# Decoder trunk on one core: x laid out by features, key/query before gates, unit matrix moved by 96 bytes

## The chip, the cores and the metric

The kernel runs on one core of one Trainium2 chip. The time is device microseconds of one execution, the median of three runs. A separate execution was profiled; it has its own time and a span, which is the part between the first and the last instruction that the profiler recorded. Engines are called TensorE (PE, with PEld for its weight loads), VectorE (DVE), ScalarE (ACT), GpSimd (POOL) and SyncE (SP, which here only starts transfers).

## The reference, cut to what matters

Two decoder layers on 256 tokens of 2048 features, all in float32: a gated DeltaNet mixer, a SwiGLU network, an HGRN2 mixer, a SwiGLU network, and a last norm. The change touches how the first mixer begins:

```python
h = x
h = h + gdn_mixer(rmsnorm(h, gdn_norm[j]), gdn_w_in[j], ...)

def gdn_mixer(h, w_in, conv_w, a_log, dt_bias, head_norm, w_out):
    proj = h @ w_in                       # q, k, v | z | b, a
    qkv = silu(causal_depthwise_conv(proj[..., :GDN_CONV_DIM], conv_w))
    ...
    beta = sigmoid(b)
    g = -exp(a_log) * softplus(a + dt_bias)
    o = gated_delta_rule_chunked(q, k, v, beta, g)
    o = rmsnorm(o, head_norm) * silu(z)
    return o @ w_out
```

The norm's weights are folded into x in front of the products (`split_scaled`), and the norm's scale of each token (rstd, one over the root of the mean square) is applied behind them.

## The kernel before, in words

**Products in three parts.** A float32 product is made of three faster ones. Each operand is split into a high part, in a shorter format, and the low rest: x into `xt_h` and `xt_l`, weights into `wh` and `wl`. TensorE then sums wh·xh, wh·xl and wl·xh. The high part is written by ScalarE (`activation` with Copy), the low part by VectorE (raw minus high).

**The stream.** All weights pass once through `stream`, in halves of 128 x 1024 numbers (512 KB): SP loads `raw` (four buffers), ScalarE writes `wh`, VectorE writes `wl` (four buffers each), TensorE multiplies. Halves are laid out in groups; a group is one set of output columns with an accumulator `main` (two of them, used in turn), and its `end` function takes the result out. A high or low part can be written only once TensorE has finished with the half four places earlier, and a group can start only once the accumulator of two groups earlier has been emptied. The order of the groups of the DeltaNet stage is the string `GDN_ORDER`: k0 is the key/query group of heads 0, then k1 and so on, v the values, z the output gate, o the output projection. In front of k0 stands the group `ba`, one half with the 64 columns of the gates b and a. A key/query half is 24 matmuls with 256 columns of x moving (`mm_cols`), a half of v, z or o is 12 matmuls with 512 columns of weights moving (`mm_rows`), and the gates' half is 48 matmuls of 256 columns (`mm_gates`).

**How x comes in.** `start` loads x in four pieces of 512 columns, tokens on partitions. TensorE transposes each piece (`make_xt`, eight transposes of 128 x 128 with the unit matrix `head` moving), ScalarE and VectorE split what comes out, scaled by the norm's weights. ScalarE sums the squares of the same pieces (`sumsq`, output in `junk`), and `make_rstd` makes the scales: a short chain over VectorE, GpSimd (power -0.5), VectorE (the scale times the unit matrix, in `vjunk`) and TensorE (`ones` times that), so that `rstd_row` holds the scales of all tokens on every partition. Ten matmuls of `ones` come first, to keep TensorE busy until x is there.

**What the groups' ends do.** `gates_end` makes decay and beta from the gates' group, a chain over VectorE, ScalarE and DRAM (`g_rows`, `g_tots`, read back on all partitions). `kq_end` empties the accumulator into `pre` times `rstd_row` (`conv_evac`), runs the convolution and its SiLU (`gdn_qk`), makes `dec`, the decay between tokens, on ScalarE in 24 pieces of 128 x 64 and one exponential over all of them, and starts the triangular inverse (`gdn_inverse`), a long chain of small VectorE steps on `u`. `z_end` calls `gdn_o`, whose matmuls are the small products `aux<-r,u`, `aux<-w,nmat` and `aux<-w,dec`; square sums of their result follow on ScalarE (`junk<-aux`), then the transposes `aux<-head,zs`.

**What sets the order.** Nothing is issued as it is written. Every operation is recorded with its inputs, outputs and an estimated cost, and `plan` lays out one order for each engine from these costs and from how late an operation may come; main matmuls keep the order of the stream, all other work is put between. `lag` is the estimated time to landing of a transfer, `edge` forces one operation behind another. All instructions are issued from one line (490), so the profile's groups are told apart by the names of their tiles.

**Where constants lie.** `setup` lays out the constants one behind the other in the order of the calls. `head`, which holds the unit matrix and the norms' weights, lies at byte 128 modulo 512 of each partition; `wh` in row groups and most work tiles lie at 32.

Of the kernel before, what the change touches and what calls it, by code (L numbers as in the profile page):

```python
# [17 lines left out]
P = 128  # L18
T = 256
# [487 lines left out]
class Trunk:  # L507
# [27 lines left out]
    def setup(self):  # L535
        nc, c = self.nc, self.const
        t = lambda shape, tag, dt=F32: self.tile(c, shape, tag, dt)
        self.x_home = self.tile(self.dram, [T, D], "x_home", bufs=1)
        self.x_at, self.x = self.a["x"], {}
        head = t([P, P + 64], "head")  # L540
        nc.sync.dma_start(head, self.a["head"])
        nc.ops[-1].lag = 2.4
        self.queue = [nc.ops[-1]]
        self.ident = head[:, 0:P]
        self.norms = head[:, P : P + 64].rearrange("p (n c) -> p n c", n=4)
        self.ones = t([P, P], "ones")
        nc.gpsimd.memset(self.ones, 1.0)
        self.neghalf = t([P, 8], "neghalf")
        nc.gpsimd.memset(self.neghalf, -0.5)
        self.rstd = t([P, 2], "rstd")  # L550
        self.rstdh = t([P, 2], "rstdh")
        self.rstd_row = t([P, T], "rstd_row")
        self.ssp = t([P, 2, 4], "ssp")
        self.ss = t([P, 2], "ss")
        self.junk = t([P, 512], "junk")
        self.vjunk = t([P, 256], "vjunk")
        self.xt_h = [t([P, 4, T], f"xt_h{i}", F32R) for i in range(4)]
        self.xt_l = [t([P, 4, T], f"xt_l{i}", F32R) for i in range(4)]

    def start(self, norm, row):  # L560

        pool = self.nc.pool("first", 1, phase=True)
        for cg in range(4):
            if cg < 2:
                self.x[cg] = self.tile(pool, [P, 2, 512], f"first{cg}")
            else:
                self.x[cg] = self.tile(self.xpool, [P, 2, 512], "x", ordered=True)
            self.nc.sync.dma_start(self.x[cg], self.x_cols(self.x_at, cg))
            self.nc.ops[-1].lag = (2.5, 2.2, 3.0, 3.0)[cg]
            self.nc.edge(self.queue[-1], self.nc.ops[-1])  # L570
            self.queue.append(self.nc.ops[-1])
        warm = self.aux()
        for i in range(10):
            self.nc.tensor.matmul(
                warm[:, (i % 4) * P : (i % 4 + 1) * P], self.ones, self.ones, start=True, stop=True
            )
        for cg in range(4):
            self.make_xt(cg, norm)
        for cg in range(4):
            self.nc.after(self.xt_h[cg])  # L580
            self.sumsq(cg)
        self.nc.close(pool)
        self.make_rstd(row)


# [1 line left out]
    def stream(self, groups):  # L587
        nc = self.nc
        flat = [(g, i) for g in groups for i in range(len(g.halves))]
        ready = {}  # L590

        def place(tag, g):
            w = self.tile(self.wsplit, [P, 1024], tag, F32R, ordered=True)
            v = nc.virtual(w)
            v.pad, v.cols = PAD, g.cols
            return w

        def load(n):
            g, i = flat[n]
            raw = self.tile(self.wraw, [P, 1024], "raw", ordered=True)  # L600
            nc.sync.dma_start(raw, g.halves[i])
            if n == 0:
                nc.ops[-1].lag = 4.2
                nc.edge(self.queue[1], nc.ops[-1])
            h = place("wh", g)
            nc.scalar.activation(h, raw, AF.Copy)
            low = place("wl", g)
            nc.vector.tensor_tensor(out=low, in0=raw, in1=h.bitcast(F32), op=ALU.subtract)
            ready[n] = (h, low)

        loaded = 0
        for n, (g, i) in enumerate(flat):
            while loaded < min(n + AHEAD, len(flat)):
                load(loaded)
                loaded += 1
            if i == 0:
# [34 lines left out]

    def mm_cols(self, ps, i, wh, wl, n_k, n_f, n_chunks):

        for k in range(n_k):
            kt = i * n_k + k
            xh, xl = self.operand(kt)
            for f in range(n_f):
                at = (k * n_f + f) * P
                for m, (w, s) in enumerate(((wh, xh), (wh, xl), (wl, xh))):
                    self.nc.tensor.matmul(  # L660
                        ps[:, f // 2, (f % 2) * T : (f % 2 + 1) * T], w[:, at : at + P], s,
                        start=(kt == 0 and m == 0 and f % 2 == 0),
                        stop=(i == 2 * n_chunks - 1 and k == n_k - 1 and m == 2),
                        skip_group_check=True,
                    )

    def mm_gates(self, ps, i, wh, wl):
        for kt in range(16):
# [573 lines left out]
    def gdn_o(self, hg, st):  # L1242
# [39 lines left out]
    def gdn(self, after):  # L1282
        a = self.a
        states = [{} for _ in range(N_HG)]
        groups = []

        def gates_end(ps):
            self.gdn_gates(ps)

        ba = Group([a["gdn_ba"]], self.mm_gates, gates_end)  # L1290
        cols = lambda chunks, end: Group(
            chunks, lambda ps, i, h, l: self.mm_cols(ps, i, h, l, 2, 4, 4), end, cols=True
        )

        def part(hg):
            st = states[hg]

            def kq_end(ps):
                self.gdn_qk(hg, self.conv_evac(ps), st)
                self.gdn_inverse(hg, st)  # L1300

            def v_end(ps):
                self.gdn_v(hg, ps, st)

            def z_end(ps):
                st["zs"] = zs = self.tile(self.pool, [P, 2, 512], "zs", bufs=2)
                for tt in range(2):
                    self.nc.scalar.activation(
                        zs[:, tt, :], ps[:, tt, :], AF.Silu, scale=self.rstd[:, tt : tt + 1]
                    )  # L1310
                self.gdn_o(hg, st)
# [12 lines left out]
        groups.insert(0, ba)  # L1324
        groups[0].begin = self.gdn_setup
        return groups

# [332 lines left out]

    def run(self):
        self.setup()
        self.start(0, True)
        groups = self.gdn(self.next_input(1, False))
        groups += self.ffn(0, self.next_input(2, True))
        groups += self.hgrn(self.next_input(3, False))
        groups += self.ffn(1, self.finish)
        self.stream(groups)
        self.leave()
# [12 lines left out]
def layout(inputs):  # L1682
    f = lambda n: np.ascontiguousarray(inputs[n])
    out = {}
    x = f("x").reshape(T, D)
    out["x"] = np.ascontiguousarray(x.reshape(2, P, 4, 512).transpose(2, 1, 0, 3))
    cols = lambda v: v.reshape(16, P).T
    ffn_norm = f("ffn_norm")
    norms = [cols(v) for v in (f("gdn_norm")[0], ffn_norm[0], f("hgrn_norm")[0], ffn_norm[1])]
# [18 lines left out]
    w = f("gdn_w_in")[0]  # L1708
# [4 lines left out]
    ba = w[:, 6 * D :].reshape(16, P, 64)  # L1713
# [47 lines left out]
```

## Time and profile before

| | us |
|---|---|
| median of three runs | 2769.14 (2768.69 to 2769.49) |
| profiled execution | 2768.12 |
| its span | 2766.0 |
| TensorE matmuls, busy | 2749.6 |
| TensorE weight loads, busy | 2333.5 |
| VectorE busy | 1899.9 |
| ScalarE busy | 1428.6 |
| GpSimd busy | 251.6 |

The granted TensorE clock of the profiled execution is 0.999 of full speed. In the rows, `out<-in` names the tiles, `x8` the number of instructions merged, and a note in brackets the idle time in front of them with what ended it. Rows of the transfers end with the median time from issue to landing. A matmul is recorded longer than the distance to the next one, since they are pipelined; the distance is what counts. Rows of a chain of waits are start, length, engine and tile. Rows of stretches give, for each engine in the order PE, PEld, DVE, ACT, POOL, its busy time, then the granted clock, the transfer engines' busy share and GB/s.

### The profile page before, as it was taken

How to read it: one execution, taken by the hardware profiler on the slowest of the kernel's cores; microseconds unless marked ns; L12 is line 12 of the kernel's file. 1: busy time of each engine (PE TensorE's matmuls, PEld its weight loads, DVE VectorE, ACT ScalarE, POOL GpSimd, SP SyncE). 2: the span in 40 equal slices, each digit the busy share in tenths (PEclk: the TensorE clock that was granted, in tenths of full speed). 3: DMA queues.
4: the chain of work that ended last, by engine and by line, in shares of the span. 5: the costliest groups of instructions: out<-in, count | busy, mean ns of one | idle time of the engine just before them, and what ended most of it. 6: DMA issues, size and time to landing. Idle time of an engine off the chain costs nothing.

```text
span 2766.0 us, 41091 instructions
## 1 busy us (share of the span) xinstructions
PE 2749.6 (99%) x15662; PEld 2333.5 (84%) x15662; DVE 1899.9 (69%) x2857; ACT 1428.6 (52%) x2010; POOL 251.6 (9%) x370
## 2 busy tenths in 40 slices
PE   9999999999999999999999999999999999999998
PEld 9888888888888888888888989988888888888887
DVE  7787888877766667446675688778657675456764
ACT  6646666565554444344444556556454444344443
POOL 1213222232110000000000100000100000000000
PEclk9999999999999999999999999999999999999999
DMA  7686668687776666676667655555776666766664
GB/s 262 201 282 222 189 213 286 205 276 218 229 254 202 193 194 194 224 223 195 192 191 224 219 163 175 168 166 176 231 258 195 193 193 209 224 208 194 195 200 160
DMA packets 162677, 580.52 MB, mean 210 GB/s; under 512 B 20138, under 2 KB 21306, under 8 KB 162352
## 3 DMA queue, kind: packets, MB, share of 16 engines
q1 hardware_dynamic: 138912, 503.15, 57.0%
q0 software_dynamic: 23280, 73.91, 8.5%
q8 instruction: 122, 2.00, 0.3%
q10 hardware_dynamic: 288, 0.85, 0.1%
q14 instruction: 75, 0.61, 0.1%
HBM read 550.52 MB, written 27.31 MB: 209 GB/s over the span
## 4 chain that ended last, share of the span: by engine, by line
PE 99%; ACT 0%; DVE 0%; issue 0%; DMA 0%; SPq 0%; POOLq 0%; POOL 0%; ACTq 0%
PE main L490 92%; PE aux L490 6%; ACT dec L490 0%; DMA first<-in_x 0%; DVE wl L490 0%; ACT wh L490 0%; DVE utmp L490 0%; SPq L490 0%; DVE pre L490 0%; ACT xt_h L490 0%; DVE u L490 0%; ACT y L490 0%; POOLq L1757 0%; ACT junk L490 0%; DVE xl L490 0%
## 5 line engine op out<-in xcount | busy, mean ns | idle before, releaser
L490 DVE TENSOR_TENSOR wl<-raw,wh 128x1024 fp32r<-128x1024 f32 x945 | 1160.7, 1229 | 755.6 <-ACT wh L490 742.2
L490 ACT ACTIVATE wh<-raw 128x1024 fp32r<-128x1024 f32 x945 | 1000.8, 1060 | 1226.9 <-PE main L490 1126.3
L490 PE MATMUL main<-wh,xt_h 128*128 128x512 f32 x2176 | 849.3, 390 | 0.8 <-ACT wh L490 0.8
L490 PE MATMUL main<-wl,xt_h 128*128 128x512 f32 x2176 | 848.4, 390 | 1.3 <-DVE wl L490 1.3
L490 PE MATMUL main<-wh,xt_l 128*128 128x512 f32 x2176 | 849.5, 390 | 0.0
L490 PEld LDWEIGHTS main<-wl,xt_h 128*128 128x128 f32 x2176 | 408.5, 188 | 85.7 <-DVE wl L490 1.6
L490 PEld LDWEIGHTS main<-wh,xt_h 128*128 128x128 f32 x2176 | 408.5, 188 | 85.0 <-ACT wh L490 1.2
L490 PEld LDWEIGHTS main<-wh,xt_l 128*128 128x128 f32 x2176 | 408.6, 188 | 84.4
L490 PE MATMUL main<-xt_h,wh 128*128 128x256 f32 (+1 forms) x1040 | 290.5, 279 | 0.7 <-ACT wh L490 0.7
L490 PE MATMUL main<-xt_h,wl 128*128 128x256 f32 (+1 forms) x1040 | 290.1, 279 | 1.0 <-DVE wl L490 0.9
L490 PE MATMUL main<-xt_l,wh 128*128 128x256 f32 (+1 forms) x1040 | 290.0, 279 | 0.3 <-DVE xt_l L490 0.3
L490 PE MATMUL main<-wh,htl 128*128 128x512 f32 x664 | 258.6, 389 | 0.0
L490 PE MATMUL main<-wl,hth 128*128 128x512 f32 x664 | 258.3, 389 | 0.0
L490 PE MATMUL main<-wh,hth 128*128 128x512 f32 x664 | 258.3, 389 | 0.0
L490 PEld LDWEIGHTS main<-xt_h,wl 128*128 128x128 f32 (+1 forms) x1040 | 194.5, 187 | 1.5 <-DVE wl L490 1.4
L490 PEld LDWEIGHTS main<-xt_h,wh 128*128 128x128 f32 (+1 forms) x1040 | 194.5, 187 | 1.3 <-ACT wh L490 0.9
L490 PEld LDWEIGHTS main<-xt_l,wh 128*128 128x128 f32 (+1 forms) x1040 | 194.5, 187 | 1.0 <-DVE xt_l L490 0.5
L490 DVE STREAM_TRANSPOSE turned<-h 32x256 f32<-32x256 f32 x352 | 153.5, 436 | 7.2
L490 PE MATMUL main<-wh,ot_l 128*128 128x512 f32 x384 | 151.2, 394 | 0.0
L490 PE MATMUL main<-wh,ot_h 128*128 128x512 f32 x384 | 150.6, 392 | 0.0
L490 PE MATMUL main<-wl,ot_h 128*128 128x512 f32 x384 | 150.5, 392 | 0.0
L490 PEld LDWEIGHTS main<-wh,hth 128*128 128x128 f32 x664 | 124.7, 188 | 25.9
(206 smaller groups left out, 2249.0 us busy)
## 6 DMA issues: line engine op xcount, KB each, us to landing
raw<-in_ffn_gu SPq DMA_DIRECT2D x352, 512.0 KB, 4.7
raw<-in_ffn_d SPq DMA_DIRECT2D x176, 512.0 KB, 4.7
raw<-in_hgrn_in SPq DMA_DIRECT2D x128, 512.0 KB, 4.1
raw<-in_gdn_kq SPq DMA_DIRECT2D x64, 512.0 KB, 5.4
raw<-in_gdn_v SPq DMA_DIRECT2D x64, 512.0 KB, 4.7
raw<-in_gdn_z SPq DMA_DIRECT2D x64, 512.0 KB, 4.9
raw<-in_gdn_out SPq DMA_DIRECT2D x64, 512.0 KB, 5.0
x_home<-x POOLq DMA_DIRECT2D x36, 512.0 KB, 6.7
```

What stands on the lines that cost most here:

```text
L490: getattr(getattr(tc.nc, op.eng), op.method)(*args, **kw)
```

## The change

It has four parts.

1. A second copy of x, laid out by features (`x_turned`), comes as an input. `start` loads it in four pieces and splits it straight away; the 32 opening transposes go, and ten warm-up matmuls become nine. The pieces of x with tokens on partitions are still loaded, for the square sums and the residual, behind the turned ones.
2. The first four halves of the stream are issued by `start`, each in front of a piece of turned x, in one forced order on SP.
3. k0 comes first in the stream and the gates' group second; of k0's end, only the emptying of the accumulator stays there, and the rest (`gdn_qk`, `gdn_inverse`) is held back until the gates' end has been recorded. In the very first half, the matmuls are sorted: all wh·xh, then all wl·xh, then all wh·xl.
4. The constants are laid out in another order, with two of them widened (`neghalf` to 72 columns, `vjunk` to 320), so that `head` lies at byte 32 modulo 512. `ones`, `junk`, `vjunk` and `rstd_row` come to lie at 288; all tiles behind the constants keep their place modulo 512.

```diff
@@ setup
+        neghalf = t([P, 72], "neghalf")
+        self.neghalf = neghalf[:, 0:8]
...
         head = t([P, P + 64], "head")
-        nc.sync.dma_start(head, self.a["head"])
-        nc.ops[-1].lag = 2.4
-        self.queue = [nc.ops[-1]]
...
+        self.vjunk = t([P, 320], "vjunk")[:, 0:256]
+        self.queue = []
+        self.in_turn(head, self.a["head"], 2.4)
...
+    opening = True
+
+    def in_turn(self, out, in_, lag):
+        self.nc.sync.dma_start(out, in_)
+        op = self.nc.ops[-1]
+        op.lag = lag
+        if self.queue:
+            self.nc.edge(self.queue[-1], op)
+        self.queue.append(op)
+
-    def start(self, norm, row):
+    def start(self, norm, row, first):
...
         for cg in range(4):
-            if cg < 2:
-                self.x[cg] = self.tile(pool, [P, 2, 512], f"first{cg}")
-            else:
-                self.x[cg] = self.tile(self.xpool, [P, 2, 512], "x", ordered=True)
-            self.nc.sync.dma_start(self.x[cg], self.x_cols(self.x_at, cg))
...
+            raw = self.tile(self.wraw, [P, 1024], "raw", ordered=True)
+            self.in_turn(raw, first[cg], 3.0)
+            self.early.append(raw)
+            turned.append(self.tile(pool, [P, 4, T], f"first{cg}"))
+            self.in_turn(turned[cg], self.a["x_turned"][cg], 3.0)
         warm = self.aux()
-        for i in range(10):
+        for i in range(9):
...
         for cg in range(4):
-            self.make_xt(cg, norm)
+            for k in range(4):
+                self.split_scaled(
+                    self.xt_h[cg][:, k, :], self.xt_l[cg][:, k, :], turned[cg][:, k, :],
+                    self.norms[:, norm, 4 * cg + k : 4 * cg + k + 1],
+                )
+        nc.close(pool)
         for cg in range(4):
-            self.nc.after(self.xt_h[cg])
+            self.x[cg] = self.tile(self.xpool, [P, 2, 512], "x", ordered=True)
+            self.in_turn(self.x[cg], self.x_cols(self.x_at, cg), 4.0)
             self.sumsq(cg)
-        self.nc.close(pool)
         self.make_rstd(row)
@@ mm_cols
+        steps = [(k, f, m) for k in range(n_k) for f in range(n_f) for m in range(3)]
+        if self.opening:
+            steps.sort(key=lambda s: -s[2] % 3)
+            self.opening = False
...
@@ gdn
         def gates_end(ps):
             self.gdn_gates(ps)
+            held.pop()()
...
             def kq_end(ps):
-                self.gdn_qk(hg, self.conv_evac(ps), st)
-                self.gdn_inverse(hg, st)
+                pre = self.conv_evac(ps)
+
+                def rest():
+                    self.gdn_qk(hg, pre, st)
+                    self.gdn_inverse(hg, st)
+
+                if hg:
+                    rest()
+                else:
+                    held.append(rest)
...
-        groups.insert(0, ba)
+        groups.insert(1, ba)
@@ run
-        self.start(0, True)
         groups = self.gdn(self.next_input(1, False))
+        self.start(0, True, groups[0].halves)
@@ layout
+    out["x_turned"] = np.ascontiguousarray(x.T.reshape(4, 4, P, T).transpose(0, 2, 1, 3))
```

More of the change, by code (lines that the diff above doesn't have):

```diff
@@ L539, in setup @@
         self.x_at, self.x = self.a["x"], {}
+        neghalf = t([P, 72], "neghalf")
+        self.neghalf = neghalf[:, 0:8]
+        self.rstd = t([P, 2], "rstd")
+        self.rstdh = t([P, 2], "rstdh")
+        self.ssp = t([P, 2, 4], "ssp")
+        self.ss = t([P, 2], "ss")
         head = t([P, P + 64], "head")
-        nc.sync.dma_start(head, self.a["head"])
-        nc.ops[-1].lag = 2.4
-        self.queue = [nc.ops[-1]]
         self.ident = head[:, 0:P]
@@ L546, in setup @@
         self.ones = t([P, P], "ones")
-        nc.gpsimd.memset(self.ones, 1.0)
[L548 to L556, printed above, removed]
+        self.rstd_row = t([P, T], "rstd_row")
@@ L557, in setup @@
+        self.junk = t([P, 512], "junk")
+        self.vjunk = t([P, 320], "vjunk")[:, 0:256]
+        self.queue = []
+        self.in_turn(head, self.a["head"], 2.4)
+        nc.gpsimd.memset(self.ones, 1.0)
+        nc.gpsimd.memset(neghalf, -0.5)
         self.xt_h = [t([P, 4, T], f"xt_h{i}", F32R) for i in range(4)]
         self.xt_l = [t([P, 4, T], f"xt_l{i}", F32R) for i in range(4)]
-    def start(self, norm, row):
-        pool = self.nc.pool("first", 1, phase=True)
-        for cg in range(4):
-            if cg < 2:
-                self.x[cg] = self.tile(pool, [P, 2, 512], f"first{cg}")
-            else:
-                self.x[cg] = self.tile(self.xpool, [P, 2, 512], "x", ordered=True)
-            self.nc.sync.dma_start(self.x[cg], self.x_cols(self.x_at, cg))
-            self.nc.ops[-1].lag = (2.5, 2.2, 3.0, 3.0)[cg]
-            self.nc.edge(self.queue[-1], self.nc.ops[-1])
-            self.queue.append(self.nc.ops[-1])
+    opening = True
@@ new lines, in in_turn @@
+    def in_turn(self, out, in_, lag):
[6 more added lines that the diff above has]
+    def start(self, norm, row, first):
+        nc = self.nc
+        pool = nc.pool("first", 1, phase=True)
+        self.early = []
+        turned = []
+        for cg in range(4):
+            raw = self.tile(self.wraw, [P, 1024], "raw", ordered=True)
[3 more added lines that the diff above has]
+            self.in_turn(turned[cg], self.a["x_turned"][cg], 3.0)
@@ L572, in start @@
         warm = self.aux()
-        for i in range(10):
-            self.nc.tensor.matmul(
+        for i in range(9):
+            nc.tensor.matmul(
                 warm[:, (i % 4) * P : (i % 4 + 1) * P], self.ones, self.ones, start=True, stop=True
@@ L599, in load @@
             g, i = flat[n]
[L600 to L604, printed above, removed]
+            if n < len(self.early):
+                raw = self.early[n]
+            else:
+                raw = self.tile(self.wraw, [P, 1024], "raw", ordered=True)
+                nc.sync.dma_start(raw, g.halves[i])
             h = place("wh", g)
@@ L652, in mm_cols @@
     def mm_cols(self, ps, i, wh, wl, n_k, n_f, n_chunks):
-        for k in range(n_k):
+        steps = [(k, f, m) for k in range(n_k) for f in range(n_f) for m in range(3)]
+        if self.opening:
+            steps.sort(key=lambda s: -s[2] % 3)
+            self.opening = False
+        for k, f, m in steps:
             kt = i * n_k + k
             xh, xl = self.operand(kt)
[L657 to L665, printed above, removed]
+            w, s = ((wh, xh), (wh, xl), (wl, xh))[m]
+            at = (k * n_f + f) * P
+            self.nc.tensor.matmul(
+                ps[:, f // 2, (f % 2) * T : (f % 2 + 1) * T], w[:, at : at + P], s,
+                start=(kt == 0 and m == 0 and f % 2 == 0),
+                stop=(i == 2 * n_chunks - 1 and k == n_k - 1 and m == 2),
+                skip_group_check=True,
+            )
     def mm_gates(self, ps, i, wh, wl):
@@ L1285, in gdn @@
         groups = []
+        held = []
         def gates_end(ps):
             self.gdn_gates(ps)
+            held.pop()()
         ba = Group([a["gdn_ba"]], self.mm_gates, gates_end)
@@ L1298, in kq_end @@
             def kq_end(ps):
-                self.gdn_qk(hg, self.conv_evac(ps), st)
-                self.gdn_inverse(hg, st)
+                pre = self.conv_evac(ps)
[4 more added lines that the diff above has]
+                    rest()
+                else:
+                    held.append(rest)
             def v_end(ps):
```

## The prediction

> **What bounds the kernel now.** I read the page first, then the busy time by stretches, the chain of waits through the opening, and the timelines of the engines wherever the chain leaves TensorE.
>
> ```profile
> PE 99%; ACT 0%; DVE 0%; issue 0%; DMA 0%; SPq 0%; POOLq 0%; POOL 0%; ACTq 0%
> ```
> ```profile
> 5.00:40.00 35.00, 33.37 (x288) 32.62 (x287) 23.79 (x39) 26.91 (x50) 9.76 (x20) 1.00 0.88 311
> ```
> ```profile
> 280.00:400.00 120.00, 116.28 (x873) 102.62 (x872) 99.02 (x246) 79.63 (x160) 27.01 (x40) 1.00 0.64 197
> ```
>
> TensorE sets the end. It loses time only at the start (its first work on x begins at 5.50), in the opening (1.6 us idle), around 300 and 390 us (3.7 us idle), and at the tail, which the change does not touch. So the change is worth what it takes from those holes and from TensorE's own work, less what it opens elsewhere. The opening by the chain of waits (start, length, what) and by TensorE's timeline:
>
> ```profile
> 10.45 0.87 PE aux L490 x8
> ```
> ```profile
> 16.59 16.59 PE main L490 x144
> 33.17 0.44 PE aux L490 x4
> 33.62 11.58 PE main L490 x102
> ```
> ```profile
> 1.07 4.63 PE L490 MATMUL aux<-ones 128*128 128x128 f32 x20 [1.07 <-POOL ones L490]
> 5.50 1.08 PE L490 MATMUL aux<-head,first 128*128 128x128 f32 x8
> 7.92 1.09 PE L490 MATMUL aux<-head,first 128*128 128x128 f32 x8 [1.33 <-DMA first<-in_x]
> ```
>
> Four batches of eight transposes stand in the opening, some 0.87 us each. The main stream needs 16.59/144 = 0.115 us per 256-column matmul there and 11.58/102 = 0.1135 a little later. At 16.59 two of the 48 gate matmuls are left, and the 192 of the first key/query group follow, 194 in all: 144 up to 33.17, the other 50 by 33.62 + 50 x 0.1135 = 39.3. At 39.3 the second key/query group starts. That moment is my mark for the opening, since in both kernels the same 240 matmuls lie before it.
>
> **The change part by part.**
>
> *x by features, key/query first.* The 32 transposes (4 x 0.87 = 3.5 us of TensorE) go. SP issues the unit matrix, then weight half 0, turned x 0, half 1, turned x 1, and so on: the second to fifth transfers of the queue have the same sizes as today's, so I take today's landings for them (issue rows, then issue to landing):
>
> ```profile
> 1.26 0.42 SPq L490 DMA_DIRECT2D first<-in_x  x1
> 1.73 0.43 SPq L490 DMA_DIRECT2D raw<-in_gdn_ba  x1
> 2.21 0.43 SPq L490 DMA_DIRECT2D first<-in_x  x1
> 2.68 1.05 SPq L490 DMA_DIRECT2D x<-in_x  x2
> ```
> ```profile
> first<-in_x SPq DMA_DIRECT2D x1, 512.0 KB, 3.7
> ```
> ```profile
> raw<-in_gdn_ba SPq DMA_DIRECT2D x1, 512.0 KB, 4.5
> ```
> ```profile
> first<-in_x SPq DMA_DIRECT2D x1, 512.0 KB, 5.7
> ```
> ```profile
> x<-in_x SPq DMA_DIRECT2D x1, 512.0 KB, 6.5
> ```
>
> So half 0 is there at 4.96, turned x 0 at 6.23, half 1 at 7.91, turned x 1 at 9.18, then one more every 1.3 us. The splits that follow cost what these rows say (ScalarE, ScalarE, VectorE, VectorE):
>
> ```profile
> 7.86 2.32 ACT L490 ACTIVATE xt_h<-aux,head 128x256 fp32r<-128x256 f32 x6
> ```
> ```profile
> 15.28 2.94 ACT L490 ACTIVATE wh<-raw 128x1024 fp32r<-128x1024 f32 x3
> ```
> ```profile
> 9.14 2.44 DVE L490 SCALAR_TENSOR_TENSOR xt_l<-aux,head,xt_h 128x256 fp32r<-128x256 f32 x6
> ```
> ```profile
> 16.45 3.49 DVE L490 TENSOR_TENSOR wl<-raw,wh 128x1024 fp32r<-128x1024 f32 x3
> ```
>
> A quarter-tile split is about 0.4 us on either engine, a weight split about 1.0 and 1.2. ScalarE has the high part of half 0 at 6.0 and of the first quarter of x at 6.7; TensorE starts at 6.75. The sorted first half needs 24 x 0.1145 = 2.75 us, its low parts are there in time, so it ends at 9.5. The second half waits for its low part: half 1 at 7.91, + 1.05, + 1.23 = 10.2, needed after two matmuls at 9.73, a wait of 0.5. The low parts of halves 2 and 3 come out at 13.0 and 15.7, which is when TensorE wants them; from half 4 on there is slack of 0.3 us and growing. All 240 matmuls end at 6.75 + 0.5 + 240 x 0.1145 = 34.75, against 39.3 - 0.44 (the small broadcast of the row scales is in the second) = 38.9. Up to here 4.1 us are gained.
>
> *Gates second.* This gives most of it back. There are two main accumulators. In the kernel before, the second key/query group takes the one that the gates left, emptied by a 64-row product long before. Now it takes the one of the first key/query group, which the convolution's evacuation (pre) empties, and that needs the row of scales, whose sums come from x copies now loaded last. In the compiled order TensorE broadcasts the row right behind the gates, VectorE then has the low part of weight half 12, the copy of the row, pre; and half 12 takes the buffer that the gates' half leaves, so its split starts only when the gates end. The rows:
>
> ```profile
> 33.66 0.42 DVE L490 COPY rstd_row<-aux 128x256 f32<-128x256 f32 x1 [0.73 <-PE aux L490]
> ```
> ```profile
> 39.00 1.23 DVE L490 TENSOR_TENSOR wl<-raw,wh 128x1024 fp32r<-128x1024 f32 x1
> 40.14 1.22 DVE L490 TENSOR_TENSOR pre<-main,rstd_row 128x1024 f32<-128x1024 f32 x1
> ```
> ```profile
> 39.30 1.06 ACT L490 ACTIVATE wh<-raw 128x1024 fp32r<-128x1024 f32 x1 [0.65 <-PE main L490]
> ```
>
> 34.75 + 0.1 + 1.06 (high part) + 1.23 (low part) + 0.42 (copy) + 1.22 (pre) = 38.8: TensorE idles some 3.5 us behind its broadcast, and the second key/query group starts at 38.8 instead of 39.3. This edit pair yields 0.5 us. Bounds: if half 12 did not stand in front, 34.75 + 0.44 + 0.42 + 1.22 = 36.8, a gain of 2.5; if the tight halves 1 to 3 each slip by half a transfer (0.65), 40.7, a loss of 1.4. What is hidden under the 3.5 us: the row itself. Its way today, from the last square sum to the scaled diagonals that TensorE broadcasts:
>
> ```profile
> 27.08 0.19 ACT L490 ACTIVATION_READ_ACCUMULATOR junk<-x 128x1 f32 x1
> ```
> ```profile
> 30.12 0.48 DVE L490 TENSOR_SCALAR vjunk<-head,rstd 128x128 f32<-128x128 f32 x2
> ```
>
> That is 30.60 - 27.27 = 3.3 us. By the transfers' pace x copies 2 and 3, the 18th and 20th, land around 29 and 31, with weight split 11 between their square sums; the last sum ends near 33, the diagonals come by 36.3, and the copy of the row is due only at 37.1. The gates' own chain (scan, sums to DRAM) and the first group's convolution start within 2 us of their old moments and are wanted only a hundred microseconds later: nothing.
>
> *The plan behind it.* The kernel lays out its order by a planner, so a moved start reshuffles the whole DeltaNet stage; behind it the orders are the same. I therefore looked in both compiled orders for what causes the holes at 300 and 390 us. It is a ScalarE batch of 24 decay pieces plus an exponential without a weight split in between (ScalarE; the chain of waits; TensorE's timeline at both holes):
>
> ```profile
> 292.98 5.85 ACT L490 ACTIVATE dec<-g_row,shift 128x64 f32<-128x64 f32 x24 [0.56 <-PE aux L490]
> 298.85 1.28 ACT L490 ACT_TABLE_LOAD   x1
> 300.14 1.49 ACT L490 ACTIVATE dec<-dec 128x1536 f32<-128x1536 f32 x1
> 301.53 3.88 ACT L490 ACTIVATE wh<-raw 128x1024 fp32r<-128x1024 f32 x4
> ```
> ```profile
> 290.26 2.69 PE aux L490 x24
> ```
> ```profile
> 302.62 0.39 PE L490 MATMUL main<-xt_h,wh 128*128 128x256 f32 x1 [0.69 <-ACT wh L490]
> ```
> ```profile
> 304.06 0.39 PE L490 MATMUL main<-xt_h,wl 128*128 128x256 f32 x1 [0.94 <-DVE wl L490]
> ```
> ```profile
> 391.18 0.50 PE L490 MATMUL main<-wh,xt_h 128*128 128x512 f32 x1 [0.79 <-ACT wh L490]
> 392.98 0.50 PE L490 MATMUL main<-wl,xt_h 128*128 128x512 f32 x1 [1.29 <-DVE wl L490]
> ```
>
> Let E be the end of the 24 products w,dec in front of the batch (292.95 above). The batch runs from E to E + 8.6; the next high part is done at E + 9.65, the low part at E + 10.9. TensorE lives on the matmuls that its order puts behind E. A product in front of the batch starts 2.69/24 = 0.11 behind the one before it, while one of that size lasts 0.27 in the rows of the unit matrix below: a modelled end lies about 0.16 us behind the next possible start. So the two holes cost (0.69 + 0.94 + 0.79 + 1.29) + 4 x 0.16 = 4.4 us. A 512-column matmul is worth 17.24/76 = 0.227 us by this row of the chain:
>
> ```profile
> 613.42 17.24 PE main L490 x76
> ```
>
> In the new order four batches stand alone. First (key/query group 4): 89 small matmuls behind E, to E + 10.2, low part wanted at 10.4: 0.5 us, where the old order had none. Second (group 5): 85 matmuls instead of 79, and two matmuls later 20 products of another kind that need no split: nothing left of its 1.95. Third (group 6): 8 small and 36 large ones instead of 54 and 12, to E + 9.2: 0.5 + 1.0, against 2.5. Fourth (group 7), spread over four splits until now: one plus 48 large, to E + 11.2, the batch itself 1.3 later: 0.8. Together 2.8 against 4.4, a gain of 1.6. Bounds: none of them costs (gain 4.4); all cost 2.5 (loss 5.6).
>
> *Unit matrix at byte 32.* It is the moving operand of the 194 transposes that stay. The nearest rows are products of the same width whose moving operand r lies at byte 32 already:
>
> ```profile
> L490 PE MATMUL aux<-r,u 128*128 128x128 f32 x128 | 16.8, 274 | 0.0
> ```
> ```profile
> L490 PE MATMUL aux<-head,x 128*128 128x128 f32 x112 | 14.5, 272 | 0.0
> ```
>
> 274 ns against 272: I take zero; 194 x 2 ns = 0.4 us either way bounds it. The other constants that move (ones, the scratch rows) feed no long matmul.
>
> Sum: 0.5 + 1.6 = 2.1 us, so the profiled execution would go from 2766.0 to 2763.9 of span. It took 2768.12 us, 1.02 less than the median of the runs, 2769.14; the same step from the median gives 2767.0.
>
> The row above has the warm-up matmuls of ones at 4.63/20 = 0.23 us a piece, against 2.69/24 = 0.11 for the later ones of that size, with the granted clock at 1.00 in every stretch. The Trainium skill (TensorE: Matmul & The Clock Gate, "What's actually happening") has the array start at half clock and be released after a busy window of about 3.4 us that is not tied to the kernel's start. It speaks against the change: one warm-up matmul fewer (9 for 10), and no transposes between them and the first main matmul.
>
> **The rivals.** (1) *The clock is not up yet at 6.75.* For: the warm-up ends near 5.0, and 1.7 us of nothing follow. Against: a gap of 1.33 at 7.92 today leaves no slow matmuls behind. Half rate for the 4.4 us that today lie between 1.07 and 5.50 would cost 2.2, less the 0.5 that TensorE waits anyway: 2768.7. (2) *The batches stop hurting* because the new order feeds TensorE enough: 0.5 + 4.4 = 4.9 gained, 2764.2; with half 12 out of the way besides, 6.9 gained, 2762.2. For it: the second batch loses its hole by a count of matmuls. Against: the count for the third and fourth. (3) *Slower: the batches start late.* Their first piece waits for the row from DRAM (g_row) and the shifts; the place is ScalarE at groups 4 to 7. Every microsecond of delay beyond E is paid by three batches in full and by the second after its 0.6 of slack. From 0.7 us of delay on the kernel is no longer faster (3 x 0.7 + 0.1 = 2.2 against 2.1); with 1.5 us it is 3 x 1.5 + 0.9 - 2.1 = 3.3 slower, 2772.4. Against: today's batch of the rows above starts 0.03 behind E. (4) *The start pays in full*, because the copy of the row does not wait: 2.5 + 1.6 gained, 2765.0; against it, the compiled order.
>
> **How the numbers follow.** The forecast 2767.0 has 0.5 (own range 2765.5 to 2768.5), (1) 0.12, (2) 0.16, (3) 0.12, (4) 0.10. About 0.2% (5.5 us) is what a measurement of this kernel can tell from no change. Below 2763.6 lie the better half of (2) and a little of (4): 0.12. Above 2774.7 lies only the far end of (3): 0.04. 0.84 stay within. The range leaves out the extremes of (2) and (3): 2763.0 to 2771.5.
>
> **What would show it.** Right: the first main matmul at 6.7 to 6.9 with no transposes; TensorE idle 3 to 4 us behind the broadcast at 35, with pre as the releaser and half 12's low part before the copy; the second key/query group at 38.8; holes of about 0.5, 0, 1.5 and 0.8 us behind the four batches. Wrong: early main matmuls 0.2 us apart (rival 1); a hole of 2 us or more behind each batch (rival 3); transposes below 265 ns, which I price at zero.

## The result and the profile after

The changed kernel takes 2774.27 us (median of 22 runs, 2772.36 to 2777.12), the kernel before 2769.15 (22 runs, 2767.76 to 2770.94): a ratio of 1.0020, 95% interval 1.0013 to 1.0027. It was forecast at 2767.0, between 2763.0 and 2771.5. The profiled execution took 2774.25 with a span of 2772.2, against 2768.12 and 2766.0, so the two spans differ by 6.2 us. Where they come from is read in four steps.

**The opening.** The page's shares of the chain that ended last, by engine:

```profile
PE 96%; DVE 1%; DMA 1%; ACT 1%; issue 1%; SPq 0%; POOL 0%; POOLq 0%; ACTq 0%
```

TensorE set the end for 99% before; now transfers, VectorE and ScalarE each hold it somewhere. The busy time by stretches shows where (columns as before: length, the time and count of TensorE, its weight loads, VectorE, ScalarE, GpSimd; granted clock; DMA share; GB/s):

```profile
5.00:40.00 35.00, 30.21 (x246) 29.50 (x245) 22.15 (x34) 25.87 (x46) 8.41 (x19) 0.95 1.01 376
280.00:400.00 120.00, 117.91 (x900) 105.05 (x899) 99.17 (x231) 75.09 (x152) 24.30 (x38) 1.00 0.66 209
```

TensorE is busy 3.2 us less in the first 35 us than before, the clock is at 0.95 instead of 1.00, and the DMA engines have no slack left (1.01; 0.88 before). Between 280 and 400 it idles 2.1 us, 3.7 before; one of its holes, 1.9 us at 404, now lies behind that stretch. Then TensorE's timeline, at the first main matmuls and at the second key/query group (start, length, what, idle time before and its releaser):

```profile
7.53 1.18 PE L490 MATMUL main<-xt_h,wh 128*128 128x256 f32 x8 [2.16 <-ACT xt_h L490]
...
11.61 0.41 PE L490 MATMUL main<-xt_h,wh 128*128 128x256 f32 x1
11.82 0.41 PE L490 MATMUL main<-xt_l,wh 128*128 128x256 f32 x1
...
36.34 0.28 PE L490 MATMUL main<-xt_h,wl 128*64 128x256 f32 x1
39.25 0.88 PE L490 MATMUL aux<-vjunk,ones 128*128 128x128 f32 x4 [2.64 <-DVE vjunk L490]
42.33 0.55 PE L490 MATMUL main<-xt_h,wh 128*128 128x256 f32 x1 [2.20 <-DVE pre L490]
...
45.88 0.41 PE L490 MATMUL main<-xt_l,wh 128*128 128x256 f32 x1
46.10 0.41 PE L490 MATMUL main<-xt_h,wl 128*128 128x256 f32 x1
...
46.63 0.28 PE L490 MATMUL main<-xt_h,wl 128*128 128x256 f32 x1
46.75 0.28 PE L490 MATMUL main<-xt_h,wh 128*128 128x256 f32 x1
```

The reader sees three things. The first main matmul comes at 7.53, and sixteen of those up to 12.2 stand 0.21 us apart, not 0.113. The last of the 240 starts at 36.34, but the broadcast of the row of scales waits until 39.25 and the second key/query group until 42.33 (39.3 before). And behind that pause the matmuls are 0.21 us apart again until 46.4: nineteen gaps, 2.0 us more than at 0.113. The pause is 42.33 - 36.45 = 5.9 us long, with only the broadcast in it; the granted clock is 0.50 from 39.7 to 46.4. It is also 0.50 from 9.0 to 12.3, behind the 2.16 us of idle time in front of the first main matmul. The Trainium skill (TensorE: Matmul & The Clock Gate, "What's actually happening") has the clock fall to half after an idle window of about 3.4 us; the trace has the fall, but behind less: neither 2.16 us nor the 2.64 us in front of the broadcast is as long. The chain of waits says what the pause waits for:

```profile
25.97 0.19 ACT junk L490
26.18 9.44 DMA x<-in_x
...
39.47 1.13 DVE wl L490
...
40.96 1.24 DVE pre L490
...
42.33 12.13 PE main L490 x84
```

The last x copy is issued at 26.18, when the square sums of the second one (ScalarE, junk) have given its buffer back, and takes 9.44 us in the full queues. It lands at 35.6, the scaled diagonals come at 39.4, and only then follow half 12's low part, the copy of the row and pre.

**The holes of the DeltaNet stage.** A hole is a stretch behind 43 us in which TensorE stands idle. TensorE's waits in the changed kernel (what waited, for what: us in total, times, longest), without those of the opening:

```profile
PE main L490 <- DVE wl L490: 4.7, 4, 2.1
...
PE main L490 <- DVE u L490: 1.0, 1, 1.0
PE aux L490 <- DVE zs L490: 0.9, 2, 0.6
PE main L490 <- ACT wh L490: 0.6, 1, 0.6
PE main L490 <- DVE ot_l L490: 0.5, 1, 0.5
PE main L490 <- ACT ot_h L490: 0.3, 1, 0.3
```

8.0 us in ten waits; with the 0.16 us a wait that the prediction adds, 9.6 us (9.9 from start to start, as the expectations below count them), against 4.4 before (4.5). The largest stands behind the second batch of decay pieces. The chain of waits there:

```profile
302.90 2.68 PE aux L490 x24
305.58 9.68 PE main L490 x85
...
315.29 0.04 DVE pre L490
...
316.43 0.22 DVE u L490
316.65 1.14 DVE wl L490
...
317.84 0.50 PE main L490
```

The 85 matmuls that the prediction counted are there. They end a key/query group, though, and VectorE's order has the evacuation of that group (pre) and a short product (u) ahead of the low part for the next one. So VectorE stands idle for 3.3 us until the 85 end, and only then comes to the low part: 2.6 us from the end of the 85 to 317.84, with one matmul in between.

**The HGRN stage gives time back.** One head group's stretch in the chain of waits, first of the kernel before, then of the changed one:

```profile
1658.77 0.87 PE aux L490 x8
1659.64 40.62 PE main L490 x302
```

```profile
1670.25 0.87 PE aux L490 x8
1671.13 38.91 PE main L490 x302
```

The same 302 matmuls in the same order take 1.7 us less, behind the same batch of eight transposes. TensorE's timeline in these stretches, before and after:

```profile
1665.84 0.28 PE L490 MATMUL main<-xt_h,wl 128*128 128x256 f32 x1
1665.96 0.28 PE L490 MATMUL main<-xt_h,wh 128*128 128x256 f32 x1
```

```profile
1676.75 0.28 PE L490 MATMUL main<-xt_h,wh 128*128 128x256 f32 x1
1676.86 0.28 PE L490 MATMUL main<-xt_l,wh 128*128 128x256 f32 x1
```

120 ns from start to start before, 113 after. The granted clock is 1.00 in both.

**The account.** The end of the DeltaNet stage and the end of the HGRN stage by the last batches of transposes in the chain of waits, before and then after:

```profile
827.96 32.20 PE main L490 x142
...
2041.08 58.95 PE main L490 x260
```

```profile
839.74 20.41 PE main L490 x90
...
2047.50 52.60 PE main L490 x232
```

At the first the changed kernel is 11.8 us behind: 3.0 from the later second group, 2.0 from the slow matmuls behind it, 5.2 from the holes; 1.6 are spread over the stage and not traced to a place, some 0.4 of them from matmuls 120 ns apart behind the clock's return. At the second it is 6.4 behind: 5.4 were won back.

### The profile page after: what moved, and what is told of

It reads as the page before. It is cut to its first block, busy times and chain, and to the rows that moved or that the text cites. A ratio compares the mean times of both kernels' runs of the same rounds, so it can differ in the third digit from the quotient of the medians.

```text
span 2772.2 us, 41024 instructions
## 1 busy us (share of the span) xinstructions
PE 2746.3 (99%) x15628; PEld 2327.8 (84%) x15628; DVE 1898.0 (68%) x2857; ACT 1428.9 (52%) x2010; POOL 251.2 (9%) x370
## 4 chain that ended last, share of the span: by engine, by line
PE 96%; DVE 1%; DMA 1%; ACT 1%; issue 1%; SPq 0%; POOL 0%; POOLq 0%; ACTq 0%
PE main L490 90%; PE aux L490 6%; DMA x<-in_x 1%; DVE wl L490 0%; DMA raw<-in_gdn_kq 0%; ACT wh L490 0%; ACT dec L490 0%; ACT junk L490 0%; DVE u L490 0%; DVE utmp L490 0%; SPq L490 0%; DVE pre L490 0%; DVE zs L490 0%; ACT y L490 0%; POOLq L1787 0%
## 5 line engine op out<-in xcount | busy, mean ns | idle before, releaser
L490 PEld LDWEIGHTS main<-wl,hth 128*128 128x128 f32 x664 | 124.6, 188 | 26.1
```

Source lines behind the costliest of these rows:

```text
L490: getattr(getattr(tc.nc, op.eng), op.method)(*args, **kw)
```

## The experiments

Each time is the median beside runs of the kernel before on the same chip (2768.7 to 2769.5), the ratio is to those.

**The layout alone**: the constants in the changed order on the kernel before.

```diff
+        neghalf = t([P, 72], "neghalf")
         ...
         head = t([P, P + 64], "head")
         ...
+        self.vjunk = t([P, 320], "vjunk")[:, 0:256]
```

> The kernel before with only the changed layout of the constants (unit matrix at byte 32, the block 512 bytes longer); x is still transposed and the gates still come first. Theory A, the layout sets the spacing of the 256-column main matmuls in the HGRN stage: they are about 113 ns apart all through it as in the changed kernel, and the time falls by some 5 us to about 2764. Theory B, the 120 ns stretches are a state into which TensorE falls at a switch between main and small matmuls, whatever the layout: the order and its timing are those of before, so the stretches stay, and the time is 2769 within 1 us. In both the transposes stay at 272 ns.

2763.14 us, ratio 0.9981 (0.9971 to 0.9990). The order is that of before, the stretch of 302 takes 38.91 us. The layout is worth 5.6 us, which the prediction priced at zero. So the other three parts, with the plan that comes with them, lose 10.7 (5.6 gained with the layout alone, 5.1 lost with the whole change). The two next runs ask which part of the layout it is.

**Unit matrix moved, operands of the main matmuls not; and the reverse.**

```diff
+        self.neghalf = t([P, 104], "neghalf")[:, 0:8]
         head = t([P, P + 64], "head")
         ...
-        self.neghalf = t([P, 8], "neghalf")
         ...
-        self.vjunk = t([P, 256], "vjunk")
+        self.vjunk = t([P, 416], "vjunk")[:, 0:256]
```

> The kernel before, its order unchanged, with the unit matrix alone at byte 32 modulo 512: the block of constants grows by 1024 bytes, so that the transposed x, the raw weights and the splits stand where they stood modulo 1024. In the kernel before each of the four batches of transposes in front of a 256-column run of the HGRN stage is followed by matmuls 120 ns apart up to the next batch of small matmuls, while runs behind other small matmuls go at 113. Theory A, the moving operand's place (the unit matrix) sets which it is: all runs go at 113 and the time falls by 5 to 6 us to 2763. Theory B, what counts is the place of the operands of the main matmuls: the 120 stays, 2769 within 1 us.

```diff
-        self.vjunk = t([P, 256], "vjunk")
+        self.vjunk = t([P, 384], "vjunk")[:, 0:256]
```

> The kernel before, its order unchanged, with 512 bytes behind the constants: the unit matrix stays at byte 128 modulo 512, and the transposed x, the raw weights and the splits move by 512 as they do in the changed kernel. Theory A, the unit matrix sets the spacing behind the transposes: 120 ns stays, 2769 within 1 us. Theory B, the place of the main matmuls' operands does: 113 and 2763.

2764.14 us (0.9981, 0.9972 to 0.9991) with the unit matrix moved; 2769.48 us (1.0001, 0.9992 to 1.0010) with the operands moved. The chain of waits at the same stretch, of the first and of the second:

```profile
1660.39 0.87 PE aux L490 x8
1661.26 38.91 PE main L490 x302
```

```profile
1660.94 0.87 PE aux L490 x8
1661.81 40.62 PE main L490 x302
```

The eight transposes take 0.87 us in both. What differs is the stream behind them: with the unit matrix at byte 128 it runs at 120 ns a matmul until the next batch of small ones, at byte 32 at 113. Theory A holds, with one reservation: by the code, the first edit also moves `ones`, `rstd_row`, `junk` and `vjunk` modulo 512, and no run moves these alone. The eight transposes in front of the stream read none of them, so the unit matrix is the likely cause, argued and not isolated.

**Another place for it**, byte 160.

```diff
+        self.neghalf = t([P, 8], "neghalf")
         head = t([P, P + 64], "head")
         ...
-        self.neghalf = t([P, 8], "neghalf")
```

> The kernel before, its order unchanged, with the row of constants -0.5 put ahead of the unit matrix, which so stands at byte 160 modulo 512 instead of 128; all from the norms' scales on stays where it was. Byte 128 left the 256-column runs behind transposes at 120 ns and byte 32 at 113. Theory A, 32 bytes past a multiple of 128 are enough: 113 ns, 2763 to 2764. Theory B, only the place near 32 modulo 512 does it, or 160 shares the trouble of 128: 120 ns, 2769 within 1 us.

2769.67 us (1.0001, 0.9992 to 1.0011), and 40.62 us for the stretch: 160 is like 128, theory B. `ones` moves by 32 bytes here too, to no effect. What tells 32 from them is open; three places were tried.

**The x copies with buffers of their own.**

```diff
-        nc.close(pool)
         for cg in range(4):
-            self.x[cg] = self.tile(self.xpool, [P, 2, 512], "x", ordered=True)
+            if cg < 2:
+                self.x[cg] = self.tile(pool, [P, 2, 512], f"own{cg}")
+            else:
+                self.x[cg] = self.tile(self.xpool, [P, 2, 512], "x", ordered=True)
             ...
+        nc.close(pool)
```

> The changed kernel with two more buffers for the x copies, so that copies 2 and 3 are issued without waiting for the square sums of copies 0 and 1. Theory A, the last x copies set the start of the second key/query group and the idle time there lets the clock fall: the last square sum ends near 29 instead of 37.2, TensorE does not wait for the scaled diagonals (2.6 us before), the second key/query group starts between 36.5 and 40.5 instead of 42.3, and fewer or none of the 18 matmuls behind it are 213 ns apart (1.8 us); 3 to 7 us are gained up to 60 us, 2767 to 2771 if the holes of the plan stay as they are. Rival, the low part of half 12 and the convolution's evacuation set it anyway: the group still starts at 41 or later and the gain up to 60 us is below 1.5 us.

2768.85 us (1.0000, 0.9991 to 1.0009), 5.4 under the changed kernel. The chain of waits:

```profile
35.94 0.46 PE aux L490 x4
...
36.92 1.20 DVE pre L490
...
38.25 10.90 PE main L490 x94
```

The last sum ends at 29.95, the broadcast stands among the gate matmuls, half 12 no longer stands in front of pre, and the second group starts at 38.25, 4.1 us earlier than in the changed kernel. TensorE pauses 0.5 us in front of it, and no run of slow matmuls follows: the clock stays up there. The holes of the DeltaNet stage are the same 9.9 us, but in the profiled execution the granted clock is 0.50 from 312.8 to 316, behind one of them, which it is not in the changed kernel. Theory A holds.

**More warm-up.**

```diff
-        for i in range(9):
+        for i in range(14):
```

> The changed kernel with 14 warm-up matmuls instead of 9, which reach to the first main matmul. Theory A, the early slow matmuls are hidden behind the x copies: they come 113 ns apart from the start or nearly so, the 240 matmuls end 1.5 to 2 us earlier than 36.5, but the second key/query group still starts at 42.3 within 0.5, the idle time in front of it grows by what was gained, and the time stays at 2774 within 2 us. Rival, the cold clock is on the path: the group starts 1.5 to 2 us earlier and the time falls by as much.

2776.03 us (1.0025, 1.0016 to 1.0035). Of the sixteen slow matmuls at the start two are left and the 240 end 1.1 us earlier (1.5 to 2 were expected), but the second group starts at 42.22, as theory A has it: the early clock is hidden behind the x copies. The longer pause is followed by 25 slow gaps (2.6 us) instead of 19. A granted clock of 0.98 between 720 and 800 us, 1.00 in the changed kernel, adds 1.6: it is 0.50 from 795.4 to 798.6, behind holes that the changed kernel has too. The run with the unit matrix moved shows the same at 393, with the order of the kernel before, so such a fall need not belong to an edit.

**Gates first again.**

```diff
-            held.pop()()
         ...
-                if hg:
+                if True:
         ...
-        groups.insert(1, ba)
+        groups.insert(0, ba)
         ...
-        self.start(0, True, groups[0].halves)
+        self.start(0, True, groups[0].halves + groups[1].halves)
```

> The changed kernel with the gates first again, key and query second; x still comes by features without transposes. Theory A, the order of the first two groups makes the loss at the start: no wait for the evacuation stands in front of the second key/query group, it starts between 36 and 38.5 (39.3 in the kernel before, 42.3 in the changed one), and up to 60 us the kernel is 1 to 3 us ahead of the kernel before; in all 2763 to 2771, the rest by the holes of the plan and the spacing in the HGRN stage. Rival, the late x copies hurt with the gates first as well: the second key/query group starts at 40 or later.

2771.34 us (1.0009, 1.0000 to 1.0018). Theory A fell, the rival holds. The chain of waits:

```profile
37.57 0.71 PE aux L490 x4
38.28 11.01 PE main L490 x97
```

The last square sum is late here too, at 34.4 (37.2 in the changed kernel), and TensorE waits 1.1 us for the diagonals, with 212 of the 240 matmuls done. The other 28 end near 38.28 + 28 x 0.1135 = 41.5, so the second key/query group starts 2.2 behind the kernel before and 0.8 ahead of the changed one. The gates use all of x before the first key/query half, and TensorE waits 3.3 us for its parts besides the slow matmuls. What the gates' second place costs is 2.8 us: these 0.8 and the 2.0 of slow matmuls (the medians differ by 2.9). The holes are the 9.9 us of the changed kernel, so they do not come from the gates' place.

**Gates third**, with the buffers and the warm-up.

```diff
-            held.pop()()
+            for rest in held:
+                rest()
         ...
-                if hg:
+                if hg > 1:
         ...
-        groups.insert(1, ba)
+        groups.insert(2, ba)
```

> The changed kernel with the gates third, behind the second key/query group, two more buffers for the x copies, and 14 warm-up matmuls. Theory A, the second key/query group need not wait for anything: the first main matmuls come 113 ns apart from 7.5 on, the group starts where the first 192 matmuls end, near 30, and its own end and the gates' come without an idle stretch, so that up to 60 us 8 to 9.5 us are gained on the changed kernel; if the holes of the plan stay at 9.9 us the time is 2765 to 2767. Rival, the gates so late delay the decay and open new holes: 2769 or more.

2777.78 us (1.0034, 1.0022 to 1.0047). The chain of waits:

```profile
7.74 32.11 PE main L490 x279
39.85 0.44 PE aux L490 x4
```

No pause from 7.74 to 96 us, and at 60 us it is 9.2 us ahead of the changed kernel, as theory A has it. Yet the time is the rival's: 18.2 us of holes, one of them 5.0 us at 787, in front of the last heads' transposes. Behind that one the granted clock is 0.50 from 791.8 to 798.4, about 3 us more. The opening and the plan behind it are separate terms, and the second (8.3 us of further holes and this clock) is larger than the first.

**Precedence for the splits.**

```diff
+        for op in ops:
+            if any(v.tag in IN_COLS for v in op.tiles) and op.eng in ("scalar", "vector"):
+                op.late -= 3.0
```

> The changed kernel with one line in the planner that gives the weight splits 3 us of precedence over other work of ScalarE and VectorE. In the changed kernel holes of 9.9 us stand behind 43 us; at 139 and 315 VectorE takes the evacuation of a finished group ahead of the low part that TensorE wants next. Theory A, the holes are the planner's order on VectorE and ScalarE and no need of the new start: they fall to 2 to 6 us and the time to 2767 to 2771. Rival, they lie in the work itself (batches of decay pieces, transposes of the outputs): 8 to 12 us of holes remain, 2772 to 2777.

2779.81 us (1.0036, 1.0023 to 1.0049). My theory A fell: 12.6 us of holes; those at 139 and 315 are unchanged, the same 5.0 us hole opened at 790, with the granted clock at 0.50 for 6.7 us behind it, and the second key/query group starts at 42.94, 0.6 later. The time is above the rival's 2777 as well. A precedence of 3 us does not reach the holes; why the planner has the evacuation first there was not traced.

**One constant of the planner, in both kernels.** The planner runs a clock of its own while it lays out the order.

```diff
-PE_SLACK = 1.5
+PE_SLACK = 0.8
```

> The changed kernel with one constant of its planner changed (PE_SLACK 0.8 for 1.5, the time it adds before a small matmul that waits for another engine). By the planner's own clock TensorE idles 20.0 us between 45 and 850 us in the changed kernel, 10.0 in the kernel before, 40.7 with the gates third, of which the traces show a little under half (9.9, 4.5, 18.2); with 0.8 it is 5.6. Theory A, the holes are this order's and not the change's: some 2.6 us of holes are left behind 43 us, the opening stays as it is, 2766 to 2768. Rival, the holes belong to the later start: 8 us or more stay and the time is 2772 or more.

> The kernel before with the same constant, 0.8 for 1.5; by the planner's own clock TensorE idles 7.9 us behind 45 us instead of 10.0. Theory A: holes of 3.5 us instead of 4.5, 2768 within 1 us, so that with this constant the change comes out about 1 us faster instead of 5 us slower. Rival, the constant helps both kernels alike: 2762 or below.

The changed kernel with 0.8: 2765.05 us (0.9984, 0.9975 to 0.9994), 9.2 under the changed kernel. TensorE's waits, all of them:

```profile
PE main L490 <- ACT xt_h L490: 2.8, 1, 2.8
PE aux L490 <- DVE vjunk L490: 2.7, 1, 2.7
PE main L490 <- DVE pre L490: 1.9, 1, 1.9
PE aux L490 <- POOL ones L490: 1.2, 1, 1.2
```

All four belong to the opening; the second key/query group starts at 43.07, 0.7 later than in the changed kernel. No hole is left behind it, and 9.9 - 0.7 comes to the 9.2 measured. The kernel before with 0.8: 2767.46 us (0.9993, 0.9983 to 1.0002), holes of 2.2 instead of 4.4. With this constant the change comes out 2.4 us faster, with 1.5 it is 5.1 slower. Theory A holds, only better than it expected (0 holes for 2.6). Both figures hold the layout's 5.0 to 5.6 us: the kernel before with 0.8 still runs its HGRN stream at 120 ns, the changed one at 113. Without the layout the change would, by that estimate, be about 3 us slower with 0.8 too; no run has the layout and 0.8 without the rest.

**A version that beats both**: the constant, the buffers and the 14 warm-up matmuls on the changed kernel.

> A version meant to beat both: the changed kernel with two more buffers for the x copies, 14 warm-up matmuls and the planner's constant at 0.8. By the parts: 2768.9 as measured with the buffers alone, less 10.6 - 2.6 us of holes, less 1 to 1.5 for the early matmuls at 213 ns: 2759 to 2761. Rival, the holes do not follow the planner's own clock, or the earlier first matmuls are lost in front of the second key/query group: 2764 or more.

2756.69 us (0.9953, 0.9938 to 0.9968): 12.8 under the kernel before, where the layout alone is 5.6 under it; 17.6 under the changed one, and 2.3 below what was expected. Its waits:

```profile
PE main L490 <- ACT xt_h L490: 1.6, 1, 1.6
PE aux L490 <- POOL ones L490: 1.2, 1, 1.2
PE main L490 <- DVE pre L490: 0.7, 1, 0.7
```

## Why the prediction was wrong, by its own steps

**The row of scales ("What is hidden under the 3.5 us: the row itself") failed.** I set the landing of x copies 2 and 3 "by the transfers' pace" at 29 and 31. They landed at 30.2 and 35.6: each waits for a buffer that ScalarE's sums give back, and then for a queue that is full. So the pause in front of the second group is 5.9 us, not the 4.0 between 34.75 and 38.8. With the buffers added the group starts at 38.25, near where I had it, though by another order. That TensorE runs at half the clock behind this pause was not priced at all: 2.0 us.

**The first matmul and rival 1.** Turned x 0 was there at 6.9, not 6.2, so the first main matmul came at 7.53 instead of 6.75 and at a falling clock: rival 1 was true as a mechanism (1.6 us of slow matmuls, my price 2.2). It cost nothing in the changed kernel, as more warm-up showed: the row of scales hid it. The 240 matmuls end at 36.45 instead of 34.75: 2.4 us gained up to there, for the 4.1 forecast. Start and clock together: 0.5 forecast as gained, 5.0 lost.

**"nothing left of its 1.95" failed.** Batch by batch I forecast 0.5, 0, 1.5 and 0.8; the trace has 0.95, 2.35, 1.9 and 1.1 us. The count of 85 was right for the second batch; the work in front of the low part in VectorE's order was not looked at. Two further holes, 1.2 us at 139 and 2.3 at 791, lay outside the batches that I searched. 1.6 were to be gained, 5.2 were lost.

**"Unit matrix at byte 32: I take zero" failed, on the other side.** The transposes themselves did not change, as priced. Their effect on the matmuls behind them was never in the sum, and it is 5.0 us by the run that moves it, with the rows laid out behind it. The kernel before had shown the two paces: its HGRN stream runs at 120 ns behind transposes and at 113 behind other small matmuls. I had taken 0.1135 from the opening for all 256-column matmuls.

**The rivals.** 3 had the sign and the stage but not the mechanism: the batches start on time (the second, which has the largest hole, 0.04 us behind the products that end at 305.58). 2, a DeltaNet stage without holes, did not come with the change but with another constant of the planner; 4 did not come, the copy of the row waited as the order had it.

Against the forecast the start is 5.5 us worse, the holes 6.8 and the untraced rest 1.6, the HGRN stage 5.4 better: 8.5 in all, from 2.1 faster to 6.4 slower at the end of that stage, and 6.2 at the end of the span. That the miss is not larger is luck: the term that was priced at zero came out on the good side.

## What to carry to other kernels

When an order is laid out by a planner, the change and the new plan are two terms: put the same change under a second setting of the planner (here one constant: +5.1 us became -2.4) before judging it, and measure parts that do not need each other apart: here the layout alone was better than the whole. When transfers are reordered, ask for each what frees its buffer, not only its place in the queue. And when an operand of small matmuls is moved, look at the spacing of the long stream behind them, not only at their own.

## What the runs showed of the hardware

The 256-column matmuls have two spacings at a granted clock of 1.00, 113 and 120 ns. In the HGRN stage, eight transposes with the unit matrix at byte 128 or 160 modulo 512 leave the stream behind them at 120 until the next batch of small matmuls; at byte 32 it goes at 113. In this kernel that is 5.0 us of 2769. The place alone does not decide: in the opening of the kernel before, the matmuls behind the same transposes (from 12.88 on) are 113 ns apart nearly throughout, with the unit matrix at 128; and in the changed kernel, with it at 32, the matmuls from 46.5 to the end of their run are 120 apart. Why is not known.

Pauses of TensorE were followed by a lower granted clock: 3.7 + 1.9 us with one small broadcast in between by 25 gaps at half rate (2.6 us), 2.6 + 2.2 us by 19 (2.0 us), and 0.5 us by none. The length alone does not decide this either. The same two waits of 0.79 and 1.29 us near 391 leave the clock at 1.00 in the kernel before, and in the run with the unit matrix moved, whose order is the same, it is 0.50 from 393.2 to 396.4. With the planner's constant at 0.8 it is 0.50 from 1931.2 to 1934.2 behind 5 us of 128 small matmuls without any wait. What else decides is open; 3.2 us at half rate cost some 1.6 us, so two single executions can differ by that much without a cause in the edit.
